# A fused QKV projection: the first load of x as one transfer or as three

## The chip, the core and the metric

The kernel runs on one core of one Trainium2 chip. The metric is the device time of one execution in microseconds (us), the median of several runs. The core's engines are named as in its profile: PE (TensorE, matrix products; PEld is its weight load), DVE (VectorE), ACT (ScalarE), POOL (GpSimd) and SP (SyncE, which here only issues transfers). Transfers between the large memory and the on-chip memory of 128 partitions run on 16 DMA engines.

## What is computed

```python
batch, seq, hidden = 16, 512, 768
x      # (16, 512, 768) float32
w_qkv  # (768, 2304) float32
qkv = np.matmul(x, w_qkv)
return np.stack([q, k, v], axis=0)   # the three column blocks of 768, float32
```

With the first two axes of x joined it is one product of 8192 x 768 by 768 x 2304, whose columns go to three outputs.

## The kernel before

**Tiling.** The rows of x are worked on in 32 *pairs* of row tiles; a pair `p` is 2 x 128 rows. The contraction of 768 is cut into six slices `j` of 128 (`KT = 6`). Of the 2304 columns, four blocks of 512 and a remainder of 256 are made. The two blocks on each side of the remainder form a group `q` (0 or 1). Most pairs use a scheme with sums of sub-blocks: seven products (`do(u, 1)` to `do(u, 7)`, L269) in place of eight, with sums of x made on POOL (`sums_x`) and sums of the weights made once on DVE (`sum_w`). Matrix products run on bf16 copies or on float32 in a reduced form.

**Order of the work.** The schedule is written by hand: each engine works through its instructions in the order in which the program issues them, and an instruction waits for the ones whose results it needs. So an instruction that waits holds back all that stands behind it on its engine.

**The first pairs.** Pairs 0 and 1 are treated apart from the others (L450 to L563), since the weights are still being loaded. `load_rows(p)` (L159) loads a pair with one transfer: partition `m` gets row `m` of the first row tile and row `m` of the second, 3072 bytes each, 786 KB in all. It is called for pair 0 at L453 and for pair 1 at L456. Behind them in SP's queue come the first weight block in six slices of 262 KB (`load_blocks(0, 0, 1)`, transfers of L92), the second weight block in two transfers, the remainder's columns, and pair 2's rows in eight pieces of 32 partitions each (L137). All of these are issued by SP, in this order. Each issue names a completion count; there are eight such counts that transfers use in turn, so a transfer waits at its issue until the one eight places before it has landed.

**From x to the first products.** `cast_rows(p)` (L170) makes a bf16 copy of each row tile: DVE casts its left half of columns (L165), ACT its right half (L166). `turn_rows(p)` (L177) turns each row tile on PE, in six transposes of 128 x 128 (L185) into one PSUM tile, and copies the result back to `xb`, half of it on DVE and half on ACT (L194, L192). The main sequence at L538 is:

```python
    busy(10)
    cast_rows(0)
    turn_rows(0, lambda: cast_rows(1))
    busy(2)
    cast_j(0, 0, b1[0], 0, dve)
    cast_j(0, 0, b1[0], 1, dve)
    turn_rows(1)
    for j in range(2, KT):
        cast_j(0, 0, b1[0], j, dve)
    late0 = block(0, 0, b1[0], singles)
```

`busy(n)` (L465) is `n` matmuls on a tile of zeros whose result nobody reads. `cast_j` (L471) casts one weight slice to bf16, here on DVE (L476). `block` (L480) issues the products of four row tiles with the six slices of a weight block (L496); its first group is slice 0 with the two row tiles of pair 0, its second slice 1 with the same, its third slices 0 and 1 with the two row tiles of pair 1. On PE, then, the order is: ten products of zeros, the twelve transposes of pair 0, two products of zeros, the twelve transposes of pair 1, and the first block. On DVE the casts of pair 1 stand behind the copies of pair 0's turned tiles (L194).

Of the kernel before, what the change touches and what calls it, by code (L numbers as in the profile page):

```python
# [10 lines left out]
def kernel(  # L11
# [20 lines left out]
    nc = tc.nc  # L32
    P = 128
# [20 lines left out]
    x_flat = x.rearrange("b t h -> (b t) h")  # L54
# [66 lines left out]
    xin, xf, xb, sr = {}, {}, {}, {}  # L121
# [34 lines left out]

    def load_rows(p):  # L159
        xin[p] = xin_pool.tile([P, 2, K], fp32, name="xin")  # L160
        rows = x_flat[p * 2 * P:(p + 1) * 2 * P, :]
        nc.sync.dma_start(xin[p][:], rows.rearrange("(r m) k -> m r k", m=P))  # L162

    def copy_halves(dst, src):
        nc.vector.tensor_copy(out=dst[0], in_=src[0])  # L165
# [284 lines left out]
    ND = 2  # L450
    zero = xb_pool.tile([P, CB], bf16, name="zero", tag="xb")
    nc.vector.memset(zero[:], 0.0)
    load_rows(0)  # L453
    nc.scalar.activation(tiny[:], zero[:, :1], ident)
    make_identity(nc, eye)
    load_rows(1)  # L456
    load_blocks(0, 0, 1)
    load_blocks(0, 1)
# [246 lines left out]
```

## Time and profile before

| | us |
|---|---|
| median of three runs (359.18 to 359.30) | 359.29 |
| the profiled execution | 358.81 |
| its span | 357.0 |
| PE busy | 350.6 (98%) |
| DVE busy | 264.4 (74%) |
| ACT busy | 185.0 (52%) |
| POOL busy | 177.3 (50%) |

The profile is of one execution. Its span runs from the first instruction to the last; what is not in it (1.8 us of the profiled execution) lies around it. Times in the views are counted from the span's start. An engine's busy time says how long its instructions ran, not that they were at their best; idle time of an engine that nothing waits for costs nothing. The views used below are the busy table, the chain of waits that ended last, the waits in total, the timeline of a stretch, and the DMA engines' rate in a stretch. In a line of the timeline come the start, the length, the engine, the line, the operation, and in brackets the engine's idle time before it with what ended it.

In the profile before, the granted clock of PE is 1.00 over the span, and HBM read 32.24 MB and written 75.50 MB: 302 GB/s over the span.

### The profile page before, as it was taken

The numbers are of one execution on the slowest core, as the hardware profiler recorded it, in microseconds if no ns is written. First come the engines' busy times: TensorE is split into PE (matmuls) and PEld (weight loads), VectorE is DVE, ScalarE is ACT, GpSimd is POOL, SyncE is SP. The second block draws the span as 40 slices with busy tenths as digits, with TensorE's granted clock in tenths as the row PEclk, the third lists the DMA queues.
The fourth block names the chain that finished last, engine by engine and source line by source line (L and its number), as shares of the span: only waits on it lengthen the run. The fifth ranks groups of instructions, "written<-read, shape, count | busy, mean of one in ns | idle before, by whom it ended". The sixth has DMA issues, their size and how long they took to land.

```text
span 357.0 us, 5315 instructions
## 1 busy us (share of the span) xinstructions
PE 350.6 (98%) x1757; PEld 252.1 (71%) x1776; DVE 264.4 (74%) x310; ACT 185.0 (52%) x317; POOL 177.3 (50%) x184
## 2 busy tenths in 40 slices
PE   7999999999999999999999999999999999999996
PEld 3474677768677686877768677686877768677674
DVE  3789876796877869777695877869777695876743
ACT  4587754545454553645545454553645545454553
POOL 0031773376566453665535566353665535566320
PEclk9999999999999999999999999999999999999999
DMA  7997999999999898998979899698999979887497
GB/s 296 380 353 238 325 378 340 373 317 348 308 311 340 257 361 206 347 266 285 361 197 385 227 342 307 209 402 213 347 263 307 331 196 392 225 303 280 155 380 260
DMA packets 82075, 108.10 MB, mean 303 GB/s; under 512 B 4992, under 2 KB 62080, under 8 KB 82048
## 3 DMA queue, kind: packets, MB, share of 16 engines
q1 hardware_dynamic: 75088, 102.52, 85.7%
q10 hardware_dynamic: 6960, 5.24, 5.5%
q8 instruction: 14, 0.23, 0.3%
q14 instruction: 13, 0.11, 0.1%
HBM read 32.24 MB, written 75.50 MB: 302 GB/s over the span
## 4 chain that ended last, share of the span: by engine, by line
PE 74%; POOL 15%; DVE 6%; issue 3%; DMA 2%; ACT 0%; SPq 0%
PE ps L258 56%; PE ps L321 12%; PE ps L496 6%; DVE xf L155 6%; POOL xb L205 5%; POOL s L226 3%; POOL s L225 3%; POOL s L227 3%; DMA xin<-in_x_dram 2%; PE ps L185 0%; DVE o L304 0%; ACT xc L166 0%; SPq L162 0%; DVE orem L424 0%; ACT orem L423 0%
## 5 line engine op out<-in xcount | busy, mean ns | idle before, releaser
L258 PE MATMUL ps<-t,s 128*128 128x512 f32 x720 | 177.9, 395 | 0.0
L258 PEld LDWEIGHTS ps<-t,s 128*128 128x128 f32 x720 | 135.1, 188 | 29.5
L155 DVE STREAM_TRANSPOSE xf<-xin 128x768 f32<-128x768 f32 (+1 forms) x45 | 93.3, 2075 | 4.3 <-DMA xin<-in_x_dram 4.3
L258 PE MATMUL ps<-b,xb 128*128 128x512 bf16 x343 | 81.6, 379 | 1.1
L298 DVE TENSOR_TENSOR o<-o,ps 128x512 f32<-128x512 f32 x56 | 38.5, 688 | 50.7 <-ACT o L297 50.0
L205 POOL CAST xb<-xf 128x1536 bf16<-128x1536 f32 x28 | 41.1, 1467 | 56.9 <-DVE xf L155 54.8
L225 POOL TENSOR_TENSOR s<-xf 128x384 fp32r<-128x384 f32 x29 | 31.0, 1068 | 72.9 <-DVE xf L155 71.1
L258 PEld LDWEIGHTS <-xb 128*128 128x128 bf16 x360 | 33.9, 98 | 36.7 <-issue 3.9
L304 DVE TENSOR_TENSOR o<-o,ps 128x512 f32<-128x512 f32 x60 | 41.1, 687 | 20.5 <-PE ps L258 19.4
L297 ACT ACTIVATE o<-ps 128x512 f32<-128x512 f32 x56 | 33.5, 598 | 42.1 <-PE ps L258 42.1
L258 PE MATMUL ps<-b,s 128*128 128x512 f32 x180 | 50.6, 389 | 0.0
L301 ACT ACTIVATE o<-ps 128x512 f32<-128x512 f32 x60 | 35.9, 598 | 25.2 <-PE ps L258 22.8
L378 DVE TENSOR_TENSOR o<-o,ps 128x512 f32<-128x512 f32 x78 | 47.8, 680 | 0.0
L321 PE MATMUL ps<-w_rem,xb 128*128 128x256 bf16 x384 | 47.4, 273 | 0.0
L286 ACT ACTIVATE o<-ps 128x512 f32<-128x512 f32 x60 | 35.9, 599 | 19.4 <-PE ps L258 14.0
L321 PEld LDWEIGHTS <-xb 128*128 128x128 bf16 x384 | 37.3, 98 | 11.5 <-issue 0.5
L335 ACT ACTIVATE orem<-ps 128x512 f32<-128x512 f32 x31 | 18.5, 598 | 48.3 <-PE ps L321 34.0
L258 PEld LDWEIGHTS ps<-b,s 128*128 128x128 f32 x180 | 33.8, 188 | 7.0
L226 POOL TENSOR_TENSOR s<-s,xf 128x384 fp32r<-128x384 f32 x29 | 29.5, 1018 | 2.3
L227 POOL TENSOR_TENSOR s<-xf 128x384 fp32r<-128x384 f32 x29 | 29.4, 1015 | 0.0
L229 POOL TENSOR_TENSOR s<-xf,s 128x384 fp32r<-128x384 f32 x29 | 29.2, 1008 | 0.0
L382 ACT ACTIVATE o<-ps 128x512 f32<-128x512 f32 x26 | 15.5, 598 | 17.9 <-PE ps L258 17.3
(49 smaller groups left out, 161.2 us busy)
## 6 DMA issues: line engine op xcount, KB each, us to landing
out_dram<-o SPq DMA_DIRECT2D x60, 768.0 KB, 4.6
out_dram<-o SPq DMA_DIRECT2D x75, 256.0 KB, 3.8
xin<-in_x_dram SPq DMA_DIRECT2D x88, 192.0 KB, 5.6
out_dram<-orem SPq DMA_DIRECT2D x31, 256.0 KB, 2.2
xin<-in_x_dram ACTq DMA_DIRECT2D x24, 192.0 KB, 4.4
st<-in_w_qkv_dram SPq DMA_DIRECT2D x5, 768.0 KB, 7.9
xin<-in_x_dram SPq DMA_DIRECT2D x2, 768.0 KB, 4.9
st<-in_w_qkv_dram SPq DMA_DIRECT2D x6, 256.0 KB, 6.0
```

The source lines that it names most:

```text
L155: nc.vector.transpose(turned[:, g:g + n], rows[:, g:g + n])
L205: nc.gpsimd.tensor_copy(out=xb[p][:], in_=xf[p][:])
L225: 1: lambda g: g.tensor_tensor(s[:, 1], a21, a22, op=add),
L226: 2: lambda g: g.tensor_tensor(s[:, 2], s[:, 1], a11, op=sub),
L227: 3: lambda g: g.tensor_tensor(s[:, 3], a11, a21, op=sub),
L258: nc.tensor.matmul(ps[:], lhs[j], rhs[j], start=(start and j == 0), stop=(j == KH - 1), skip_group_check=True,)
L286: nc.scalar.activation(c12, u.x[:], ident)
L298: nc.vector.tensor_tensor(c22, c22, u.y[:], op=add)
L301: nc.scalar.activation(c21, u.x[:], ident)
L304: nc.vector.tensor_tensor(c12, c12, u.y[:], op=add)
L321: nc.tensor.matmul(ps, xb[p][:, j, r * P:(r + 1) * P], w_rem[j // KH][:, j % KH, :], start=(j == 0), stop=(j == KT - 1), skip_group_check= ...
L378: dve.tensor_tensor(c, c, u.z[:], op=add)
```

## The change

Pair 0 is loaded with three transfers in place of one: rows 0 to 63 of the first row tile (partitions 0 to 63), rows 64 to 127 of it (partitions 64 to 127), and the second row tile (all 128 partitions). The bytes, their places and the engine that issues them are the same. `load_rows` takes a list of parts for this; pair 1 is loaded with one transfer as before. Casts of the first row tile now depend on the first two transfers, casts of the second on the third.

```diff
-    def load_rows(p):
+    def load_rows(p, parts=((slice(0, P), slice(0, 2)), )):
         xin[p] = xin_pool.tile([P, 2, K], fp32, name="xin")
-        rows = x_flat[p * 2 * P:(p + 1) * 2 * P, :]
-        nc.sync.dma_start(xin[p][:], rows.rearrange("(r m) k -> m r k", m=P))
+        rows = x_flat[p * 2 * P:(p + 1) * 2 * P, :].rearrange("(r m) k -> m r k", m=P)
+        for m, r in parts:
+            nc.sync.dma_start(xin[p][m, r], rows[m, r])
...
-    load_rows(0)
+    load_rows(0, [(slice(0, P // 2), 0), (slice(P // 2, P), 0), (slice(0, P), 1)])
```

## The prediction

> **What bounds the kernel now.** I read the page first: the busy table gives PE 350.6 of 357.0 us, so about 6.4 us of the span are without a matmul. Then I asked for the chain of work that ended last, from the start to 40 us, to see where those microseconds lie (start us, length us, what):
>
> ```profile
> 0.74 0.44 SPq L162
> 1.18 0.06 issue
> 1.24 5.67 DMA xin<-in_x_dram
> 6.91 0.02 issue
> 6.93 0.53 ACT xc L166
> 7.46 0.05 issue
> 7.51 0.95 PE ps L185 x12
> 8.46 2.82 PE ps L496 x13
> 11.28 0.05 issue
> 11.33 7.50 PE ps L496 x34
> ```
>
> The chain runs through the second of the two loads of L162, x's second pair of row tiles (I call it x1; the first load, which the change splits, is x0). It is issued at 1.24 us and landed at 6.91. ACT casts it, PE turns it, and from 7.51 on PE goes through. The waits of PE over the whole run hold two entries only:
>
> ```profile
> PE ps L469 <- DVE zero L452: 1.2, 1, 1.2
> PE ps L185 <- ACT xc L166: 0.6, 1, 0.6
> ```
>
> So after the second group of transposes nothing makes PE wait for as much as a tenth of a microsecond. Whatever moves that start, moves the end by as much: the term to find is the landing of x1.
>
> Next the timeline from 4.9 to 9.2 us, for what stands around that landing:
>
> ```profile
> 4.97 0.63 DVE L165 CAST xc<-xin 128x384 bf16<-128x384 f32 x2 [3.84 <-DMA xin<-in_x_dram]
> 5.55 0.95 PE L185 MATMUL ps<-eye,xc 128*128 128x128 bf16 x12
> 6.12 0.77 DVE L194 COPY xb<-ps 128x384 bf16<-128x384 bf16 x2 [0.52 <-PE ps L185]
> 6.93 0.94 ACT L166 ACTIVATE xc<-xin 128x384 bf16<-128x384 f32 x2 [1.02 <-DMA xin<-in_x_dram]
> 8.26 0.43 DVE L476 CAST b<-st 128x512 bf16<-128x512 f32 x1 [0.27 <-DMA st<-in_w_qkv_dram]
> ```
>
> ACT sat idle for 1.02 us until x1 landed. DVE had just finished the copies of x0's turned tiles (6.12 + 0.77 = 6.89). And x0 itself is not what PE waits for: its ten warm-up matmuls (L469) last from 1.19 to 5.49, and x0's transposes start at 5.55.
>
> Last, what the transfers do. Three windows of the DMA view: from 1.8 to 2.7 us (x0's first bytes), from 6.95 to 10.1 (weights, into all 128 partitions), and from 17.2 to 18.6 (pieces of x by L137, each into 32 partitions):
>
> ```profile
> DMA packets 40, 0.12 MB, mean 137 GB/s; under 512 B 0, under 2 KB 0, under 8 KB 40
> ...
> DMA packets 704, 1.28 MB, mean 406 GB/s; under 512 B 79, under 2 KB 79, under 8 KB 704
> ...
> DMA packets 513, 0.35 MB, mean 252 GB/s; under 512 B 53, under 2 KB 513, under 8 KB 513
> ```
>
> The reader is to see that transfers begin slowly, then fill the queue at about 406 GB/s without a hole, and that the pieces which go into a quarter of the partitions move at 252 GB/s. In 17.2 to 18.6 the windows view puts the DMA share at 1.13, so these pieces are not slow for want of work. A second such stretch, 28.7 to 30 us, moves 336 GB/s, with the engines just as full.
>
> **The change, part by part.** *Two more issues on SP.* x0 becomes three transfers: rows 0-63 and rows 64-127 of the first row tile (196.6 KB each) and the second row tile (393.2 KB). An issue of L162 or L92 holds SP for about 0.45 us and 0.05 lies between two, so x1 is issued at about 2.24 instead of 1.24, and each of the first weight transfers is 1.0 us later too. In the trace the first bytes of x0 move at about 1.8, 1.1 us after its issue. So x1's bytes can move from 2.24 + 1.1 = 3.3. They are not due before x0's 0.786 MB are through: 0.12 MB until 2.7, the rest at 404 GB/s (the rate from 2.7 to 4.5), 1.65 us, so 4.35. That covers x1's issue by 1.0 us, and the weights by more (first one ready at 3.85, due at 4.35 + 0.786/0.406 = 6.3). Cost: 0, hidden behind bytes already queued. If the queue ran dry there, it would cost up to 1.0 us.
>
> *The waits on SP.* The transfers share eight completion counts in turn, so each waits for the one eight places before. Before, the ninth (L92, first half of the second weight block) was issued at 4.96, as x0 landed. Now x0's three and x1 take four of the eight counts: the weight slices j = 4 and j = 5 wait for x0's halves, and that block's first half for the second row tile. SP would reach j = 4 at about 4.8, j = 5 at 5.3 and the block at 5.8, when the halves have long landed and the tile (5.4, below) too. The block's bytes are due behind the six slices, at 6.3 + 1.57/0.406 = 10.2. Its other half still waits for x1, and from there every transfer waits for the same one as before. Cost: 0.
>
> *Earlier casts of x0.* The casts of the first row tile no longer wait for the second. PE does not take them up earlier: ten warm-up matmuls until 5.49, transposes at 5.55, so at most 0.06 there, and nothing of it on the path, since PE's next stop is x1. Gain: 0.
>
> *The halves' rate.* This is the one term on the path. x1 lies behind x0 in the same queue, so x1 and all weights land as much later as x0's three transfers take longer than the one. There is no transfer into 64 partitions in this trace. The nearest rows: into 128 partitions, 406 GB/s; into 32, 252 and 336 GB/s. One half of 196.6 KB then takes 0.48 us, 0.78 us or 0.59 us. Lower end: no loss, 0. Upper end by rows: both halves at 252, 2 x 0.30 = 0.60. I take 252 GB/s, because that stretch is a run of such pieces back to back in one queue, two to each half of the partitions, as here; in the faster stretch they stand behind a mixed queue. But the first half does not pay all of its 0.30. The first 0.9 us move 0.12 MB whatever is asked for, so 0.12 of its 0.197 MB fall there, and only 0.074 MB are left: 0.29 us at 252 against 0.18 at 404, a loss of 0.11. The second half loses 0.30. Sum 0.41 us.
>
> Here the Trainium skill speaks against the change ("SBUF — State Buffer", section "Door 1: The DMA port swizzle"): partitions 0 to 63 reach the same 8 of 16 ports as 0 to 31, with about 218 GB/s; its section "Can I just issue two DMAs to hit both halves?" says that a second transfer does not make up for it. By that figure, an estimate from the page, each half takes 0.90 us, and both without cover 0.84 more. The row of 252 GB/s for 32 partitions agrees in kind; no row here has 64.
>
> *What follows.* ACT's cast, the transposes and PE's first blocks keep their lengths and start 0.41 later. DVE's copies of x0 stay clear: the second row tile lands at about 4.95 + 0.41 = 5.36, its casts and transposes end near their old times, the copies at about 6.9, before x1's 7.32. The weights are late by the same 0.41, and so is the matmul that needs the slice j = 1 (cast from 8.26 on, after 0.27 of waiting for it): no new wait.
>
> **Sum.** The profiled execution took 358.81 us, 357.0 of it span and 1.8 around it; the median of the runs shown is 359.29, 0.48 above it. The change adds 0.41 to the span: 357.0 + 0.41 + 1.8 = 359.2 for an execution like the profiled one, 359.7 against the median. That is +0.11%. A measurement of this kernel tells about 0.2%, 0.72 us, from no change.
>
> **The rivals.** *Slower: the halves pay in full.* If x0's slow beginning is a delay before each engine's first packets, to which the narrow rate is added, and the narrow rate is below 252 GB/s, nothing is covered. At 252 the loss is 0.60 (359.9); the slowest slices of the stretch from 17.2 to 18.6, about 200 GB/s, give 0.98 - 0.48 = 0.50 for each half, 1.0 together: 360.3. It decides, with more than 0.72, below 0.393/(0.97 + 0.72) = 233 GB/s with no cover. For it: nothing shows that the slow beginning is fixed in time. Against it: both measured stretches are faster than that.
>
> *No loss.* Two transfers one behind the other could fill both halves of the partitions together, since some engines run ahead of others in the queue; the 336 GB/s row speaks for that, since it is hard to have with a narrow limit alone. Then 0 to 0.2: 359.3 to 359.5. Against it: x0 lands as one block, and its engines cannot be far apart at the start.
>
> *Faster.* If shorter transfers begin better, up to the 0.59 us are to be had that the slow beginning costs (0.9 us less 0.12/0.406), but DVE's copies of x0 would then be in the way: they end at 6.89, at best 0.06 earlier, and behind them DVE needs 0.36 for its first cast of x1; transposes from 7.2 instead of 7.51, a gain of 0.3: 359.0. This can't reach 0.72.
>
> *PE's clock.* Ten warm-up matmuls take 4.30 us, 0.43 each; L496's 13 take 0.22 each, so PE became faster after some 4 us of work. A later x1 lengthens PE's pause before the transposes from 0.6 us to 1.0. If that pause sent PE back to the slow rate for as long as it took at first, 4 us of matmuls would cost 2 us: 361.7. Against it: the pause of 0.6 did nothing of the kind. The Trainium skill ("TensorE: Matmul & The Clock Gate", Part 1) puts the fall at an idle window of about 3.4 us, longer than any pause here.
>
> **How the numbers follow.** Forecast, a loss of 0.2 to 0.72: 0.50. Halves in full, over 0.72: 0.25. No loss, -0.1 to 0.2: 0.16. Clock: 0.05. Faster by 0.1 or more: 0.04, of which 0.02 beyond 0.72 (a cause I don't see). Slower by over 0.2%: 0.25 + 0.05 = 0.30; faster: 0.02; the rest, 0.68, within. Range: from 359.2 (no loss) to 360.3 (200 GB/s, no cover); left out are the clock, part of the faster case and what lies beyond 200 GB/s, about 0.15.
>
> **What would show it.** x1's cast on ACT starts at about 7.3 instead of 6.93, and PE's wait for it is 1.0 instead of 0.6; the rate in 2.7 to 4 us falls from 404 towards 250 GB/s; casts of x0's first row tile start before 4.97; PE has no new wait. If x1 lands at 6.9, the halves cost nothing; if at 7.7 or later, they pay in full; if L496's first matmuls take 0.43, it is the clock. If SP's next issues leave a hole in the DMA share between 3 and 6 us, my cover for the issues is wrong.

## The result and the profile after

The changed kernel takes 362.93 us (median of five runs, 360.70 to 363.94) against 359.29 (359.18 to 359.33): 1.0098 times as long, with an interval of 1.0072 to 1.0124. (This ratio and those below are estimated over all executions; they are not the quotient of two medians.) The forecast was 359.7 within 359.2 to 360.3, and "within 0.2%" as the likeliest outcome. The time lies outside the range, and the spread of the runs, 3.2 us where before had 0.15, is large as well (before had 0.7 to 1.1 us in the later rounds). The profiled execution of the changed kernel took 363.37 us with a span of 361.6, 4.6 more than the span before.

The chain of waits of the changed kernel from the start to 40 us (start us, length us, what); it answers to the first fence of the prediction:

```profile
0.74 0.59 SPq L163
...
1.38 0.57 SPq L163
...
2.00 0.58 SPq L163
...
2.63 7.07 DMA xin<-in_x_dram
...
9.72 0.53 ACT xc L167
...
10.29 1.25 PE ps L186 x12
11.55 11.71 PE ps L497 x48
```

The same chain as before, in the same order: x1, ACT's cast, the transposes, PE. But x1, issued at 2.63 instead of 1.24, landed at about 9.70 instead of 6.91. The prediction had 7.32. PE's waits over the whole run:

```profile
PE ps L186 <- ACT xc L167: 3.9, 3, 3.3
PE ps L470 <- DVE zero L453: 1.2, 1, 1.2
```

The first entry is three waits: two of 0.3 us for the casts of x0, off the path, and the long one for x1. No other wait of a tenth of a microsecond appears, so PE waits for nothing else once x1 is there. Windows of the DMA engines and PE's clock, in the windows view (columns: stretch, length, busy time and instructions of PE, PEld, DVE, ACT and POOL, granted clock, DMA share, GB/s). The changed kernel:

```profile
2.70:4.00 1.30, 1.30 (x4) 0.45 (x3) 0.00 (x0) 0.00 (x0) 0.00 (x0) 1.00 0.90 267
4.90:6.70 1.80, 1.26 (x14) 0.87 (x14) 0.85 (x4) 0.71 (x2) 0.00 (x0) 1.00 0.97 336
...
10.80:14.10 3.30, 3.30 (x14) 1.58 (x14) 2.58 (x8) 1.49 (x4) 0.00 (x0) 0.50 1.05 400
14.20:20.00 5.80, 5.80 (x28) 2.65 (x27) 4.31 (x5) 3.16 (x7) 0.00 (x0) 1.00 1.08 324
```

and the kernel before in the first two of them:

```profile
2.70:4.00 1.30, 1.30 (x4) 0.45 (x3) 0.00 (x0) 0.00 (x0) 0.00 (x0) 1.00 1.00 402
4.90:6.70 1.80, 1.74 (x16) 0.87 (x14) 1.15 (x4) 0.94 (x2) 0.00 (x0) 1.00 1.03 409
```

Three things are to be seen. While the halves move, the rate is 267 GB/s instead of 402. While x1 moves, from 4.9 us on, it is 336 instead of 409, and that was not forecast. And from 10.74 to 14.16 us, by the trace's clock records, PE had half its clock. The column of the clock is to be read with care at the start: it shows 1.00 in the first of these stretches, where a matmul of zeros took 0.43 us, twice its later 0.22. A profile's clock records begin only where PE becomes fast, at 5.22 us before and at 3.92 in the changed kernel, and ahead of that the column tells nothing.

The trace also has the sixteen completions of each transfer, one for each DMA engine. The second row tile of x0 completed between 5.10 and 5.38 us; x0 had done so by 4.95 before, so this is 0.43 later. x1's completions came between 6.36 and 6.91 before. In the changed kernel the first comes at 6.97, twelve have come by 7.43, and the last four at 8.02, 8.15, 8.88 and 9.69. A cast waits for all sixteen. So twelve engines were done near the 7.32 of the prediction, and the greater part of the loss is in the last four.

So the 4.6 us of the span are: 0.43 that everything behind the halves is late; 2.79 - 0.43 = 2.36 for the four engines that lag (ACT's cast starts at 9.72 instead of 6.93); and half of 3.41 us, 1.71, for the clock. Together 4.5; 0.1 is left over.

### The profile page after: what moved, and what is told of

It reads as the page before. It is cut to its first block, busy times and chain, and to the rows that moved or that the text cites. A ratio compares the mean times of both kernels' runs of the same rounds, so it can differ in the third digit from the quotient of the medians.

```text
span 361.6 us, 5338 instructions
## 1 busy us (share of the span) xinstructions
PE 353.0 (98%) x1776; PEld 252.5 (70%) x1776; DVE 264.5 (73%) x310; ACT 185.6 (51%) x317; POOL 177.3 (49%) x184
## 4 chain that ended last, share of the span: by engine, by line
PE 96%; DMA 2%; SPq 0%; ACT 0%; issue 0%; DVE 0%
PE ps L259 78%; PE ps L322 12%; PE ps L497 6%; DMA xin<-in_x_dram 2%; SPq L163 0%; PE ps L186 0%; ACT xc L167 0%; DVE orem L425 0%; ACT orem L424 0%
## 5 line engine op out<-in xcount | busy, mean ns | idle before, releaser
L259 PE MATMUL ps<-b,xb 128*128 128x512 bf16 x360 | 85.4, 379 | 0.0
```

Source lines behind the costliest of these rows:

```text
L259: nc.tensor.matmul(ps[:], lhs[j], rhs[j], start=(start and j == 0), stop=(j == KH - 1), skip_group_check=True,)
```

## The experiments

The kernel before was timed beside each run; its medians lie between 358.88 and 359.17 us. "x1's cast" is the start of ACT's cast of x1, 6.93 before and 9.72 with the change. The edits that name parts of x0 or x1, and the one with `busy`, are made in the changed kernel, the others in the kernel before. Times within a run are those of its one profiled execution.

**Is it the halves, or any cut?** Theory A: transfers into half of the partitions set the engines apart. Theory B: every further transfer ahead of x1 makes it late.

x0 in two transfers, one for each row tile:

```diff
-    load_rows(0, [(slice(0, P // 2), 0), (slice(P // 2, P), 0), (slice(0, P), 1)])
+    load_rows(0, [(slice(0, P), 0), (slice(0, P), 1)])
```

> x0 in two transfers, one for each row tile, both into all 128 partitions. Theory A, transfers into half of the partitions put the DMA engines out of step and x1 waits for the last engine: nothing of it here, 359.1 to 359.6 us, x1's cast on ACT at 6.9 to 7.1, first to last engine of x1 about 0.5 us apart. Theory B, each transfer more ahead of x1 makes it late, whatever its shape: one more instead of two, about half of the lateness of the change, 360 to 361.5, x1's cast at 7.6 to 8.5.

Measured: 361.38 us (360.46 to 361.80), ratio 1.0053 (1.0035 to 1.0071); x1 issued at 1.66, its cast at 8.31. No transfer here goes into half of the partitions, and x1 is late by 1.4 us. Both numbers are within those of theory B.

x0 in three transfers of the change's bytes, all into 128 partitions:

```diff
...
+            nc.sync.dma_start(xin[p][m, r, k], rows[m, r, k])
...
+    load_rows(0, [(slice(0, P), 0, slice(0, K // 2)), (slice(0, P), 0, slice(K // 2, K)), (slice(0, P), 1)])
```

> x0 in three transfers as in the change and of the same bytes, but the first row tile is cut by columns (384 and 384), so that all go into 128 partitions. Theory A: as before, 359.1 to 359.8. Theory B: as the change, 361 to 364, with x1's cast on ACT near 9 us and PE's wait for it over 2 us.

Measured: 361.50 us (360.73 to 362.66), ratio 1.0067 (1.0042 to 1.0093); x1's cast at 8.55. Theory A falls with these two, since x1 is late without any transfer into half of the partitions. Theory B's number was met in the time, less in the lateness, and PE waited 1.9 us and not over 2. The second row tile of x0, the third transfer here, issued at 1.66, is itself late: it completes between 4.61 and 6.38, where x0 before was done at 4.95.

Both transfers of x0 into halves:

```diff
+    load_rows(0, [(slice(0, P // 2), slice(0, 2)), (slice(P // 2, P), slice(0, 2))])
```

> x0 in two transfers, rows 0 to 63 of both row tiles and rows 64 to 127 of both; 393 KB each, both into half of the partitions. Theory A: at least as late as the change, since twice the bytes go into halves, 361.5 to 364.5, x1's cast at 8.5 us or later. Theory B: one transfer more, 360 to 361.5.

Measured: 361.88 us (361.51 to 362.32), ratio 1.0076 (1.0061 to 1.0091); x1's cast at 9.08. This run shows the halves' rate by itself, since from 3.3 to 5.0 us nothing else moves (windows view, columns as above):

```profile
3.30:5.00 1.70, 1.70 (x5) 0.60 (x4) 0.00 (x0) 0.00 (x0) 0.00 (x0) 1.00 1.05 240
```

With the engines full, 240 GB/s: the rate that the prediction took from the 32-partition pieces (252) is about right for 64 partitions. The Trainium skill ("SBUF — State Buffer", section "Door 1: The DMA port swizzle") states that 64 partitions are no faster than 32; these two rates agree with it, and its 218 is a little low for these two transfers one behind the other.

The time lies within theory A's range and above theory B's 360 to 361.5, but that doesn't speak for A: x0 itself, all of it moved at the halves' rate, completed only at 6.74, and PE's clock records begin at 10.23 in this profile. Until then a transpose took 0.107 us, where before took 0.056.

**The clock.** The changed kernel with ten matmuls of zeros in place of two between the two groups of transposes:

```diff
-    busy(2)
+    busy(10)
     cast_j(0, 0, b1[0], 0, dve)
```

> The changed kernel with ten matmuls of zeros between the two groups of transposes instead of two, so that PE works until about 8.5 us. If the half clock from 10.74 us for 3.41 us in the profile of the change comes from PE's long pause, it is gone and the time falls by about 1.7 us, to 360.7 to 361.8, with x1 as late as in the change. If the pause does not cause it, 362.5 to 364 with the clock low as before.

Measured: 361.87 us (361.37 to 362.78), ratio 1.0078 (1.0060 to 1.0095). x1's cast comes at 8.94, late as ever. The median is just above its range (360.7 to 361.8). The same two stretches as above:

```profile
10.80:14.10 3.30, 3.30 (x17) 1.51 (x16) 1.96 (x6) 0.87 (x2) 0.00 (x0) 1.00 1.05 408
14.20:20.00 5.80, 5.80 (x28) 2.62 (x27) 4.49 (x5) 3.72 (x7) 0.00 (x0) 1.00 1.09 327
```

The granted clock is 1.00 where it was 0.50, and its mean over the run lies between 0.998 and 1.000 in all four executions, where the change has 0.991 to 0.995 in four of five. (The fifth, with 1.000, is the one of 360.70 us.) So the half clock follows from PE's pause. The median fell by 1.06 us, less than the 1.7 of one such stretch; x1's lateness varies from run to run, and no profile separates the two in the medians.

**Does x0 have to be cut at all?** Theory D: the cutting does it, by pieces with few packets for each engine. Against B: x0 whole, and two transfers of 64 bytes to a partition between it and x1.

```diff
...
+    small = [w_pool.tile([P, 16], fp32, name=f"small{n}") for n in range(2)]
+    def load_small(n):
+        nc.sync.dma_start(small[n][:], w_qkv[n * P:(n + 1) * P, :16])
...
+    load_small(0)
+    load_small(1)
     load_rows(1)
```

> x0 whole, as before, and between it and x1 two transfers of 64 bytes to each partition into tiles that nobody reads; x1 is issued 1.0 us later and stands third behind x0, as in the change, but x0 isn't cut. Theory B, more issues and completions ahead of x1 make it late: as the change, 360.7 to 363.5, x1's cast at 8 us or later, packets over 300 ns among x1's. Theory D, the cutting of x0 itself does it (its first pieces give each DMA engine few packets, and the engines fall out of step): 359.1 to 359.7, x1's cast near 7.1.

Measured: 363.04 us (362.64 to 363.58), ratio 1.0113 (1.0098 to 1.0128): the whole loss of the change, without a cut. Its chain of waits:

```profile
0.74 0.44 SPq L167
...
1.24 0.45 SPq L78
...
1.74 0.42 SPq L78
...
2.21 6.85 DMA xin<-in_x_dram
...
9.08 0.53 ACT xc L171
```

x0 lands at 5.00, as before, and x1, issued at 2.21, at 9.06. Theory D falls.

The same small transfer, one, ahead of x0:

```diff
+    load_small(0)
     load_rows(0)
```

> x0 whole, with one such small transfer ahead of it, so that the first transfer of the kernel is short but x0 isn't cut. Theory B: one more ahead of x1, 360 to 361.5. Theory D in the form that the kernel's first transfer must be long: 360.5 to 362, as the cut by row tiles. Theory D in the form that x0's cut matters: x0 and x1 later by at most 0.5 us for the issue, 359.3 to 359.9.

Measured: 360.64 us (360.44 to 361.33), ratio 1.0049 (1.0034 to 1.0064). x1's cast at 7.44, later by no more than the issue, with x1 issued 0.47 us behind x0. The time grew by more than that: PE also waits later, for casts of pair 2's x and of the remainder's weights, 0.3 and 0.2 us, which I had not forecast. So the time lies in theory B's range, but not in its way: the one more transfer did not make x1 later than its own issue.

x0 in two transfers, each of both row tiles and half of the columns:

```diff
...
+    load_rows(0, [(slice(0, P), slice(0, 2), slice(0, K // 2)), (slice(0, P), slice(0, 2), slice(K // 2, K))])
```

> x0 in two transfers, each of both row tiles and half of the columns, so that each has 16 packets for each engine like the whole x0, of 1536 bytes. Theory B: one more transfer, as the cut by row tiles, 360.4 to 361.8. Theory D (few packets in the first piece): as before, 359.1 to 359.8. If the order in which rows of one tile are read did it, also as before.

Measured: 360.86 us, with runs from 358.84 to 362.31, ratio 1.0046 (1.0015 to 1.0077); in the profiled one (362.31) x1 was issued at 1.74 and cast at 8.76. One execution (358.84) was as fast as before: in this kernel the loss is a matter of chance in each execution.

x0 whole, x1 cut as the change cuts x0:

```diff
+    load_rows(0)
...
+    load_rows(1, [(slice(0, P // 2), 0), (slice(P // 2, P), 0), (slice(0, P), 1)])
```

> x0 whole, x1 cut as the change cuts x0: two halves of the first row tile and the second row tile. The halves' rate alone makes x1's last part 0.4 to 0.8 us later: 359.7 to 360.1. Theory B: x1's last part has two more transfers ahead of it, 360.7 to 363. Theory D: cutting a load behind one that has filled the queues does nothing more than the halves' rate: 359.7 to 360.1.

Measured: 360.06 us (359.60 to 360.68), ratio 1.0032 (1.0021 to 1.0044); the cast of x1's second row tile at 7.89. The first piece is issued at 1.22, the last at 2.46. This is the mildest of the cut kernels, near the upper end of what the halves' rate was to cost and below theory B's 360.7.

**Is it the number of transfers or the time of the issue?** Theory E: the time of x1's issue decides. Theory F: the transfers ahead of it do.

x0 and x1 whole and next to each other, but x1's issue waits for a one-column write of ACT into its tile:

```diff
...
+        if late:
+            nc.scalar.activation(xin[p][:, 0, :1], zero[:, :1], ident)
...
-    load_rows(1)
+    load_rows(1, True)
```

> x0 whole and nothing between it and x1, but x1's issue waits for a one-column write that ACT makes into its tile after the table load, so that x1 is issued at about 2.3 us as in the change (2.63), and the weights behind it late by as much. Theory E, the time of x1's issue decides (the DMA engines must have x1's work before x0's runs low): as the change, 360.7 to 363.5, packets of over 300 ns from 4 us on. Theory F, the number of transfers ahead of x1 decides: 359.1 to 359.6, x1's cast near 7.

Measured: 361.27 us (360.42 to 362.20), ratio 1.0069 (1.0046 to 1.0092); x1 issued at 2.35, its cast at 8.32. Nothing stands between the two loads, so a late issue alone is enough. The windows view of this run, around the place where x0's bytes end:

```profile
3.60:4.20 0.60, 0.60 (x3) 0.20 (x2) 0.00 (x0) 0.00 (x0) 0.00 (x0) 1.00 1.22 420
4.40:5.20 0.80, 0.75 (x3) 0.10 (x1) 0.17 (x1) 0.18 (x1) 0.00 (x0) 1.00 0.56 146
5.40:6.00 0.60, 0.40 (x6) 0.40 (x6) 0.25 (x1) 0.56 (x2) 0.00 (x0) 1.00 0.96 317
```

and of the kernel before:

```profile
3.60:4.20 0.60, 0.60 (x3) 0.20 (x2) 0.00 (x0) 0.00 (x0) 0.00 (x0) 1.00 1.04 420
4.40:5.20 0.80, 0.80 (x3) 0.15 (x1) 0.23 (x1) 0.23 (x1) 0.00 (x0) 1.00 1.03 407
5.40:6.00 0.60, 0.54 (x8) 0.44 (x8) 0.20 (x1) 0.51 (x2) 0.00 (x0) 1.00 1.04 423
```

This is the hole that the prediction named as the sign that its cover for the issues is wrong: at 4.4 to 5.2 us the engines are busy for 0.56 of the time and move 146 GB/s, 2.1 to 2.9 us after x1's issue. In the changed kernel itself there is no such hole: in the same stretch its engines are busy for 0.96 of the time and move 319 GB/s.

The counter-run: the two small transfers behind x1.

```diff
     load_rows(1)
+    load_small(0)
+    load_small(1)
```

> The two small transfers of 64 bytes to a partition stand behind x1 instead of ahead of it, so x1 is issued at 1.24 us as before, and the weights 1.0 us later than before. Theory E: x1's cast near 6.9 to 7.2, 359.1 to 359.8. Theory F: the same for x1. If late issues of the weights alone bring the long packets, x1 lands on time but the weight slices late, PE waits for their casts, and the time is over 360.

Measured: x1 issued at 1.25, its cast at 7.18, its sixteen completions within 0.45 us, no packet of x1 over 300 ns. In the same windows:

```profile
3.60:4.20 0.60, 0.60 (x3) 0.20 (x2) 0.00 (x0) 0.00 (x0) 0.00 (x0) 1.00 1.03 420
4.40:5.20 0.80, 0.80 (x3) 0.15 (x1) 0.12 (x1) 0.12 (x1) 0.00 (x0) 1.00 1.05 422
```

No hole. Theory F expects the same of this run; it falls with the run that waits for ACT, so for x1 the two together leave E. But the time is 361.99 us (361.91 to 362.19), ratio 1.0082 (1.0067 to 1.0097), because PE waits for later weights:

```profile
PE ps L326 <- DVE w_rem L566: 0.8, 1, 0.8
PE ps L190 <- ACT xc L171: 0.7, 1, 0.7
PE ps L503 <- DVE both L483: 0.6, 1, 0.6
PE ps L326 <- POOL w_rem L567: 0.2, 1, 0.2
```

The two small transfers take two of the eight counts, so the sixth weight slice waits at its issue for x1 and is issued at 7.17 instead of 4.37. The remainder's columns were issued at 9.08 instead of 8.26; their completions came between 18.05 and 20.33 us instead of 16.67 and 17.26, so here the engines are set apart as well. These waits are 1.7 us more than before's; the span grew by 3.2, and where the rest lies is not shown. My expectation for the time of this run, 359.1 to 359.8, was wrong by that.

The change with its halves issued by ACT, so that SP issues x1 at 1.19:

```diff
...
+        for m, r, *eng in parts:
+            (eng[0] if eng else nc.sync).dma_start(xin[p][m, r], rows[m, r])
...
+    load_rows(0, [(slice(0, P // 2), 0, nc.scalar), (slice(P // 2, P), 0, nc.scalar), (slice(0, P), 1)])
```

> x0 cut as in the change, but the two halves are issued by ACT and the second row tile and x1 by SP, so that x1 is issued at about 1.2 us as before, behind the same three pieces. Theory E: no long packets; x1's cast at 6.9 to 7.7, the rest being the halves' rate, 359.2 to 360.0. Theory F: three transfers ahead of x1 as in the change, 360.7 to 363.5.

Measured: 363.87 us (363.56 to 364.35), ratio 1.0135 (1.0119 to 1.0151). x1 completes at 8.73, but the second half of x0 only at 8.90, since the two queues share the engines and the halves moved beside x1 and the first weights. All casts wait for that half. PE stood still from 5.6 to 9.56, and its clock records begin only at 13.77: up to there the transposes took 0.107 us each and the first products 0.43, so a slow PE is part of this time. The run says nothing on E or F; it shows that here a second queue gave up the order of the transfers.

**What makes a late issue slow?** Two runs, with x0 whole. In the first, two weight slices are issued between x0 and x1, so that x1 is issued late but has more bytes ahead of it:

```diff
...
                 load_w(t[:, j:j + nj], j, nj, Q_OFF[q] + c * CB, CB)
+                if nj == 1 and j == 1:
+                    load_rows(1)
...
-    load_rows(1)
```

> x0 whole; the first two weight slices (0.52 MB) are issued between x0 and x1, so that x1 is issued at 2.2 us, as late as in the run where it waits for ACT, but has 1.3 us more of bytes ahead of it. Theory E in the form that the queue must not run low (x1's issue to its full flow takes some 2.5 us): no fall of the rate at 4 to 5 us, x1's engines within 0.6 us of each other, x1's cast at 8.1 to 8.4, time 359.29 + 1.3, 360.2 to 360.9. If a late issue alone, whatever lies ahead, makes x1 slow: x1's cast at 9 us or later, 361.3 or more.

Measured: 362.37 us (360.92 to 362.56), ratio 1.0083 (1.0058 to 1.0108). x1 was issued at 2.20; its completions came between 7.98 and 8.80, its cast at 8.82. The engines are 0.8 us apart instead of the 1.7 of the run that waits for ACT, and the rate at 4.5 to 5.25 is 407 GB/s instead of 152. So more bytes ahead close the hole. But x1 was to be cast at 8.1 to 8.4: of its packets that started between 5.56 and 6.42, where they begin, thirteen took 320 to 500 ns instead of 121, and the stretch from 5.9 to 6.5 moves 283 GB/s. The time is above its range for the clock: three of the four executions have a mean clock of 0.995, and the one with 1.000 took 360.92.

In the second, x1's issue waits for a fill by DVE, placed like the write of ACT above, and comes at 1.70:

```diff
...
+            nc.vector.memset(xin[p][:, 0, :512], 0.0)
...
-    load_rows(1)
+    load_rows(1, True)
```

> x0 whole; x1's issue waits for a fill of part of its tile by DVE and comes at about 1.7 us, half-way between before (1.24) and the run that waits for ACT (2.35), and as in the cut by row tiles (1.66), without its additional transfer. Queue must not run low: x0's bytes last until 4.35, 2.65 us after this issue, so x1's cast at 6.9 to 7.3 and 359.0 to 359.7. If the cut by row tiles was late (cast at 8.3) for its issue time alone, the same here: 360.4 to 361.8; if not, the cut itself or the third transfer adds to it.

Measured: 361.17 us, with six runs from 358.97 to 361.92, ratio 1.0048 (1.0021 to 1.0076). In the profiled run x1's cast is at 8.24: fifteen engines complete x1 by 6.88, as before, and one at 8.15. Two executions, 358.97 and 359.48, show nothing of it. Issued at 1.70, the load is as late as in the cut by row tiles (issued 1.66, cast 8.31), so neither the cut nor the third transfer adds anything that can be seen in these two profiles.

## Why the prediction was wrong

*Where the bound lies*: right. x1's landing sets PE's start, and PE has no later wait of a tenth; what x1 lost, the span lost, and the clock's 1.7 us on top of it.

*The halves' rate, +0.41 us*: right in kind, and in size with some luck. x0's last completion moved from 4.95 to 5.38, 0.43, and the halves move at 240 GB/s by themselves, where the sum took 252. But the first 0.9 us, in which the sum let 0.12 MB pass "whatever is asked for", passed 0.18 MB, and what was won there was lost behind it. In the run with ten matmuls of zeros, which loads x0 in the same way, the last completion came at 5.90, 0.95 later than before. So the term differs between executions, and a size like the 0.6 to 1.0 us of the rival "the halves pay in full" occurs too.

*Two more issues on SP, cost 0*: this is the step that failed. It held x1's later issue to be hidden behind bytes already queued; the runs show that a later issue alone makes x1 late, and in the profile of the change the lateness beyond the halves' rate was 2.36 us. Two of its figures were off. The three issues of x0 took 0.59, 0.57 and 0.58 us and not 0.45, so x1 was issued at 2.63 and not at 2.24. And the cover was measured from the wrong event: I took 1.1 us, from x0's issue to its first packet, as the time after which a transfer flows. But x0, issued at 0.74, flows fully only from 2.7 on, some 2.0 us later. Taken with 2.0 us, x1 issued at 2.63 flows at 4.6 and x0's bytes end at 4.35 + 0.41 = 4.8: the cover is 0.2 us, not 1.0.

Put right in this way, the sum still gives no loss. With x1 issued at 1.70 it leaves 4.35 - 3.7 = 0.65 us of cover, and four of six executions were late. What it lacks is that a load completes with its slowest engine: it moves all of x1 by one amount, while in the change twelve engines were done by 7.43 and four came up to 2.3 us behind them. What the experiments show is less than a sum: issued at 1.24 or 1.25, or at 1.66 but only 0.47 us behind x0, x1 is on time; at 1.66 to 1.74 with x0 at 0.74, late in most executions but not in all (two of six at 1.70 and one of five at 1.74 were as fast as before); at 2.1 or later, late in each profile, and less so with more bytes ahead. (With x1 cut in three, only its last piece was issued as late, at 2.46, and little more than the halves' rate was lost.) The sentence "If the queue ran dry there, it would cost up to 1.0 us" came near the mechanism and gave it no chance of its own; but in the change the engines stayed busy for 0.97 of the time from 4.9 to 6.7 us.

*PE's clock*: given 0.05 and 2 us; by the mean clock it came in four of five executions, with 1.71 us in the profiled one. The sign that the prediction gave is there: the first products (L497) took 0.43 us each until 13.9. I had priced it for a pause of 1.0 us, which the failed step made 3.3. I also leaned on the threshold in the Trainium skill ("TensorE: Matmul & The Clock Gate", Part 1), an idle window of about 3.4 us. The measurements differ: in the cut by row tiles PE paused from 6.86 to 8.89, 2.0 us, and lost the clock all the same,

```profile
6.80:8.80 2.00, 0.06 (x1) 0.00 (x0) 0.51 (x3) 0.49 (x2) 0.00 (x0) 1.00 1.00 369
9.20:12.50 3.30, 3.30 (x17) 1.67 (x15) 2.60 (x8) 1.67 (x5) 0.00 (x0) 0.50 1.05 405
```

while in the profile of the run that waits for ACT nearly the same pause, from 6.98 to 8.91, left it alone:

```profile
6.90:8.80 1.90, 0.09 (x1) 0.00 (x0) 0.45 (x3) 0.47 (x2) 0.00 (x0) 1.00 1.02 380
9.20:12.50 3.30, 3.30 (x24) 1.74 (x22) 2.54 (x8) 1.69 (x5) 0.00 (x0) 1.00 1.04 392
```

The clock records show what sets the two apart. In each profile the clock changes only at points that lie whole multiples of 3.41 us from each other, and where these points lie differs from one execution to the next. In the cut by row tiles the whole pause fell into one such step, from 5.75 to 9.17, in which PE worked for 1.38 us. In the other a step ended at 7.93, within the pause, and PE worked for 2.01 and 2.44 us of the two. In all fifteen profiles every step at full clock with 1.49 us of work or less was followed by half clock, and every one with 2.01 or more was not; none lies between.

*Waits on SP, earlier casts*: as forecast, no cost and no gain that the views show. SP did reach the weight slice j = 4 only at 6.03 and not at 4.8, because the issue before it held SP for 1.39 us. The casts of the first row tile began at 4.56 instead of 4.97, and PE's transposes at 5.14 instead of 5.55. That is more than the 0.06 that the prediction allowed: its ten warm-up matmuls ended at 4.85 and not at 5.49, since PE's clock had risen at 3.92. Nothing on the path follows from it.

What stays open is why a late start sets the sixteen engines apart, so that x1's completions lie 0.8 to 2.7 us apart instead of 0.55. That the engines run out of packets is shown by the hole of the run that waits for ACT; but in the run with the small transfers between, the engines are busy from 4.4 to 5.2 us (share 1.02) and move only 169 GB/s, with five packets of 800 to 1450 ns, and in the run issued at 1.70 a single engine lags with only two packets of x1 over 280 ns. Long packets alone do not make a load late either: with x1 cut in three, twenty took 285 to 844 ns between 4.1 and 6.3 us. In four of the late profiles (the change, the cuts by row tiles and by columns of both tiles, and the issue at 1.70) one weight issue from about 3.6 to 4.6 us on held SP for 1.15 to 1.39 us; before, none up to 5.3 us took over 0.63. Whether that is a cause or a consequence is not shown. No run here tells what such an engine waits for. None of the versions is faster than the kernel before.

## What to carry to other kernels

When issues are added ahead of a load on the critical path, compare the time from its issue until it flows at the full rate (here some 2 us, seen at the kernel's first load) with the bytes that are still queued ahead of it; the first packet is too early a mark. Keep a margin: here 0.65 us of cover by this sum was not enough in four of six executions. A load completes with its slowest DMA engine, so look at the first and the last of its completions, not at the mean rate. And a pause of PE of 2 us can halve its clock for 3.4 us, which costs 1.7, so price a longer pause together with what caused it.

## What the runs showed of the hardware

- An issue into 64 partitions held its engine for 0.55 to 0.73 us. The issue of a load into 128 partitions right behind two of them took 0.58 or 0.59; all other loads of x0 and x1 into 128 partitions took 0.37 to 0.46.
- A packet of 3072 bytes takes 121 ns in a transfer into 128 partitions. Where only transfers into 64 partitions move (3.3 to 5.0 us of the run with both transfers into halves), the median is 220.
- Some packets at the start of a late load take 300 to 1450 ns, as at the start of the kernel (up to 590 in the kernel before).
- The lateness differs between executions: the same kernel with x1 issued at 1.70 us ran in 358.97 and in 361.92 us.
- PE's clock changed only in steps of 3.41 us. A step at full clock with up to 1.49 us of work was followed by half clock, one with 2.01 or more was not.
